# First layer's S5 preparation split into input operators and output tables in a two-layer hybrid backbone kernel

## The chip, the cores and the metric

One core of a Trainium2 (trn2) chip runs the whole kernel as one launch. The metric is the device time of a launch in microseconds (us). A core has TensorE (PE, with its weight loads listed apart as PEld), VectorE (DVE), ScalarE (ACT), GpSimd (POOL) and SyncE (SP); here SP issues every DMA. Each engine works through its own instruction stream in order.

## The reference

Two layers, each run over 640 tokens (128 context tokens and 512 latent ones), width 1024. A layer computes `h = x*(1+scale)+shift`, projects `h` to an S5 input `u`, to q/k/v of two attentions and to three gates, and merges three branches:

- branch A, a bidirectional S5: 32 groups of 16 channels, 64 complex states per group and direction, `state[t] = lam_bar*state[t-1] + b_bar*u[t]`, `y[t] = Re(c*state[t]) + d*u[t]`, both directions summed, then GELU and a gated linear unit. Context and latent tokens are separate sequences; the latent one starts from a given state.
- branch B, banded attention (distance up to 128, with a sink logit), 8 query heads on 2 key heads.
- branch C, global attention with RMS-normalised q and k.

`x = LayerNorm(alpha*x + gate1*(merged @ w_out))`, and then an MLP with squared ReLU of width 4096 and a second LayerNorm. Outputs are both token sets, the context's final S5 states and its keys and values.

## The kernel before, in words

**Matmuls.** Nearly all products are made from fp32r halves: `split` (L115 to L124) writes a high part on ACT (L123) and a low part on DVE (L124), and three matmuls make one product (`mm_fm` L159 to L161, `mm_tm` L170 to L172). Weights arrive as 512 KB tiles `raw` (four buffers, L114).

**Order of the work.** The kernel is written as one long program, but the tile framework is told to schedule it: a planner walks a simulated timeline, takes for each engine the instruction that is earliest in the program among those it believes ready, and so fixes each engine's order ahead of the run. The place in the program is therefore a priority. On the chip the order of an engine never changes; an instruction that is late holds everything behind it on its engine. Buffers of a pool tag (`bufs=`) are handed out in the same way.

**The S5 in chunks of 8 tokens.** There are 84 chunk columns (`NCH`). Per block of 4 groups (8 blocks) the kernel needs three tables that depend on the parameters alone: the *input operator* (8 tokens of `u` to a state increment), the *output table* `ct` (state to 8 tokens of `y`), and the *lag kernel* (`u` to `y` inside a chunk). `s5_prep` (L274) makes them:

- once: `lam_bar` and its powers 0 to 8 by some 130 DVE operations on 128x32, the factors `fr`, `fi`, and `ec`, `ei` (L400 to L405); loads of `dP` and `delta` (L407, L409). Then a `yield`.
- per block, first half (L413 to L471): `Bm`, `Cm` loaded by two DMAs (L419, L420); `Bb` by six DVE operations of 128x64 and a sign change of `Cm` (recorded at the helper lines L290 and L294); `ct` by six DVE operations of 128x512 (L445 to L447, L451 to L453), stored to DRAM (L454); `Bs`, a padded copy of `Bb`, by a POOL memset and three DVE copies (L457 to L460); 32 small matmuls (L465, L467) into a PSUM bank `p_pt` (two buffers); 16 columns of `KK` by DVE (L468), 128 by ACT (L469). Then a `yield`.
- per block, second half (L473 to L485): the input operator, six DVE operations of 128x512 (recorded at L290), eight PE transposes (L479), two ACT copies (L480). In layer 0 it is used at once (`s5_in`), in layer 1 stored to DRAM (`inop_d`). Then a `yield`.
- at the end: 8 DMAs of `KK` into `kk_d` (L487, L488), and 8 DMAs that turn `kk_d` into the lag tables `mg_d` (L490).

`s5_in` (L588): per block 2x4 matmuls (L596); ACT writes the forward half of the chunk states `st` (L598), DVE the reversed half in two copies (L600).

**Phase A of layer 0** (`phase_a`, L494): modulation, `h`, the `u` projection, with 8 steps of the preparation after tile 1 and 8 after tile 3 (`PREP`, L26, used at L628); then `kv_gemm(0)`, `q_gemm(0)`, `kv_gemm(1)`; `s5_states` (L633): pair sums on DVE (`pairs`, L660, L661), then a recurrence of 31 steps of four POOL operations (L677 to L680), pair sums again, reversal (L689 to L691); then the banded attention: `keys(0)`, and per 128 queries `attend` (scores L915 to L920, maximum L926, exponential L938, transposes L947, split, products L954 and L955). After it in the program: the q projection of the global attention (L785, L717 to L719), 7 tiles of gates ahead (`AHEAD`), the S5 output (L1016 to L1030: loads `mg` and `ct`, the latter as `tab` with three buffers, matmuls L1023 and L1025), and the rest of the phase. The queries of the next tile are split at L870 to L873.

**Layer 1** has its preparation made during the MLP of layer 0: `ahead` (52 calls in `up` and `down`) takes a step alternately of the modulation (25 steps with its last) and of `s5_prep` (18 with its last).

Of the kernel before, what the change touches and what calls it, by code (L numbers as in the profile page):

```python
# [24 lines left out]
UA = 3  # L25
PREP = (0, 8, 0, 8)  # L26
AFF = 0
# [3 lines left out]
def net(tc, I, O, depth=DEPTH, dbg=None):  # L31
# [221 lines left out]
    def hacts(h):  # L253
        return [tuple(tuple(z[:, k] for z in p) for p in h) for k in range(8)]
# [18 lines left out]

    def s5_prep(l, pp, after=None, use=None):  # L274
        pq = ppt
# [13 lines left out]
        def tt(o, a, b, op):  # L289
            V.tensor_tensor(o, a, b, op=op)  # L290
# [108 lines left out]

        ec = pp.tile([128, 2, 8, 32], F32, name=f"ec_{l}")  # L400
        ei = pp.tile([128, 2, 8, 32], F32, name=f"ei_{l}")
# [3 lines left out]
        V.tensor_copy(ei[64:128], Pw[64:128, :, 0:8, :])  # L405
        dP = pp.tile([128, 8], F32, name=f"dP_{l}")
        SY.dma_start(dP, I["ssm_d"][:, l])  # L407
        delta = pp.tile([128, 16], F32, name=f"delta_{l}")
        SY.dma_start(delta, I["delta"])  # L409
        KK = pp.tile([128, 8, 144], F32, name=f"KK_{l}")  # L410
        yield
        for b in range(8):
            gs = slice(4 * b, 4 * b + 4)  # L413

            def pt(name, shape, bufs=1):
                return pp.tile(shape, F32, name=name, tag=f"{name}_{l}", bufs=bufs)

            Bm, Cm = pt("Bm", [128, 2, 4, 16], 2), pt("Cm", [128, 2, 4, 16], 2)
            SY.dma_start(Bm, I["ssm_b"][l, :, :, gs])  # L419
            SY.dma_start(Cm, I["ssm_c"][l, :, :, gs])  # L420
            Bb, bt = pt("Bb", [128, 2, 4, 16]), pt("bt", [128, 4, 16])
            frb, fib = (f[:, gs].unsqueeze(2).to_broadcast([128, 4, 16]) for f in (fr, fi))
            tt(Bb[:, 0], Bm[:, 0], frb, ALU.mult)
            tt(bt, Bm[:, 1], fib, ALU.mult)
            tt(Bb[:, 0], Bb[:, 0], bt, ALU.subtract)
            tt(Bb[:, 1], Bm[:, 1], frb, ALU.mult)
            tt(bt, Bm[:, 0], fib, ALU.mult)
            tt(Bb[:, 1], Bb[:, 1], bt, ALU.add)
            ts(Cm[:, 1], Cm[:, 1], -1.0, None, ALU.mult)

            def vw(t, r_):
                return t[:, r_].unsqueeze(2).to_broadcast([128, 4, 8, 16])

            def ew(t, r_):
                return t[:, r_, :, gs].rearrange("p t g -> p g t").unsqueeze(3).to_broadcast([128, 4, 8, 16])

            def row():
                r = pp.tile([128, D], F32, name="prow", tag="row", bufs=3 if l else 6)
                return r.rearrange("p (r q t o) -> p r q t o", r=2, q=4, t=8)

            mm, ct = row(), row()
            m1, m2 = mm[:, 0], mm[:, 1]


            V.tensor_tensor(m1, vw(Cm, 0), ew(ec, 0), op=ALU.mult)  # L445
            V.tensor_tensor(m2, vw(Cm, 1), ew(ec, 1), op=ALU.mult)
            V.tensor_tensor(ct[:, 0], m1, m2, op=ALU.add)  # L447
            nn = row()
            n1, n2 = nn[:, 0], nn[:, 1]
            PE_ = V  # L450
            PE_.tensor_tensor(n1, vw(Cm, 1), ew(ec, 0), op=ALU.mult)  # L451
            PE_.tensor_tensor(n2, vw(Cm, 0), ew(ec, 1), op=ALU.mult)
            PE_.tensor_tensor(ct[:, 1], n1, n2, op=ALU.subtract)  # L453
            SY.dma_start(ctab_d[l][b], ct)  # L454

            Bs = pt("Bs", [128, 2, 4, 48])
            G.memset(Bs, 0.0)  # L457
            V.tensor_copy(Bs[:, :, :, 0:16], Bb)
            V.tensor_copy(Bs[0:64, :, :, 16:32], Bb[0:64])
            V.tensor_copy(Bs[64:128, :, :, 32:48], Bb[64:128])  # L460
            p = pq()
            for q in range(4):
                o = p[32 * q:32 * q + 32]
                for r_ in range(2):
                    T.matmul(o[:, 0:16], Bs[:, r_, q, 0:32], Cm[:, r_, q, :], start=(r_ == 0), stop=(r_ == 1))  # L465
                for r_ in range(2):
                    T.matmul(o[:, 16:144], Bs[:, r_, q, 16:48], ct[:, r_, q], start=(r_ == 0), stop=(r_ == 1))  # L467
            V.scalar_tensor_tensor(KK[:, b, 0:16], delta, dP[:, b:b + 1], p[:, 0:16], op0=ALU.mult, op1=ALU.add)  # L468
            S.activation(KK[:, b, 16:144], p[:, 16:144], AF.Copy)  # L469
            yield  # L470

            io = row().rearrange("p r q t o -> p r q (t o)")
            for r_ in range(2):  # L473
                tt(n1, vw(Bb, 0), ew(ei, r_), ALU.mult)
                tt(n2, vw(Bb, 1), ew(ei, 1 - r_), ALU.mult)
# [10 lines left out]
        for q in range(4):  # L486
            SY.dma_start(ap(kk_d[l], q * 3840 + 7 * 16, [[240, 16], [4 * 3840, 8], [1, 128]]), KK[32 * q:32 * q + 16, :, 0:128])  # L487
            SY.dma_start(ap(kk_d[l], q * 3840, [[240, 16], [4 * 3840, 8], [1, 112]]), KK[32 * q + 16:32 * q + 32, :, 32:144])  # L488
        for j in range(8):
# [3 lines left out]
    def phase_a(l, h):  # L493
        if l == 0:  # L494
            pp0 = tc.alloc_tile_pool(name="prep", bufs=1, side="right", reuse_waits="tile")
            s5_use = []
            prep = s5_prep(0, pp0, use=s5_use)
        qp = tc.alloc_tile_pool(name=f"qp{l}", bufs=1, reuse_waits="tile")
# [77 lines left out]
        st = sp.tile([128, NCH, 2, 32], F32, name="st")  # L576
        segs = ((0, 18), (18, 84))
        ubs = {}

# [8 lines left out]
        def s5_in(b, io):  # L588

            if b % 2 == 0:  # L590
                ubs[0] = load_u(b // 2)
            ub = ubs[0]
            for r_ in range(2):
                p = psc()
                for q in range(4):
                    T.matmul(p[:, q * NCH:(q + 1) * NCH], io[:, r_, q], ub[:, (b % 2) * 4 + q], start=True, stop=True)  # L596
                v = p[:, :4 * NCH].rearrange("p (g c) -> p c g", g=4)
                S.activation(st[0:64, 1:NCH, r_, 4 * b:4 * b + 4], v[0:64, 0:NCH - 1], AF.Copy)  # L598
                for a, e in segs:
                    V.tensor_copy(st[64:128, a + 1:e, r_, 4 * b:4 * b + 4], v[64:128, e - 1:a:-1])  # L600

# [31 lines left out]
        def s5_states():  # L633

            for b in range(8) if l > 0 else ():
                io = sp.tile([128, 2, 4, 128], F32, name="tab", tag="tab", bufs=3)
                SY.dma_start(io, inop_d[l][b])
                s5_in(b, io)
# [371 lines left out]
        for b in range(8):  # L1010
# [5 lines left out]
            SY.dma_start(mg, mg_d[l][:, 4 * b:4 * b + 4])  # L1016
            ct = sp.tile([128, 2, 4, 128], F32, name="tab", tag="tab", bufs=3)
            SY.dma_start(ct, ctab_d[l][b])
# [14 lines left out]
        T.matmul(fp[0:64, 0:128], fin, ident, start=True, stop=True)  # L1033
        fo = sp.tile([128, 1024], F32, name="fo", tag="tab", bufs=3)[0:64, 0:128]
        S.activation(fo, fp[0:64, 0:128], AF.Copy)
# [3 lines left out]
        SY.dma_start(yT, ap(y_d[l], 0, [[8 * NCH, 128], [128 * 8 * NCH, 4], [NCH, 8], [1, NCH]]))  # L1039
        atp[0].release()  # L1040
        sp.release()
        k0p.release()
# [122 lines left out]
    def phase_b(l, M):  # L1165
# [87 lines left out]
        for t in range(NT):  # L1253
# [6 lines left out]
            build_h(l, 1, h, t, x[:, t], mp)  # L1260
        h2 = hacts(h)
        nxt = []
        if l + 1 < depth:
            nxt = [mods_steps(l + 1, range(3), lambda: mp.tile([128, 512], F32, name="mtmp", tag="mtmp", bufs=1),
                              lambda: mp.tile([128, 4, 128], F32, name="hf", tag="hf", bufs=2).rearrange("p a b -> p (a b)")), s5_prep(l + 1, mp, x[:, NT - 1, D - 1:D])]
        calls = [0]
# [223 lines left out]
```

## Time and profile before

| what | us |
|---|---|
| median of three runs (lowest, highest) | 2383.68 (2381.09, 2385.68) |
| the profiled execution's own time | 2382.53 |
| its span, first to last instruction | 2380.7 |
| PE busy in the span | 2269.5 (95%) |
| DVE, ACT, POOL busy | 1493.8, 992.7, 159.8 |

The span and the profiled execution's time differ by 1.8 us of start and end. Shares are averages over stages with different limits; PE is the engine that is nearly always busy, and a stage is read by where PE stands idle or runs at a lower granted clock. Rows of later sections come from a trace of this execution, with times from the start of the span.

### The profile page before, as it was taken

To read this page: it belongs to the slowest core of one execution; us is meant where nothing else is said; L and a number is where in the kernel's file an instruction comes from. 1 tells how busy PE (TensorE), PEld (TensorE's weight loads), DVE (VectorE), ACT (ScalarE), POOL (GpSimd) and SP (SyncE) were. 2 spreads that over 40 slices of the span, in tenths; PEclk is the share of its full clock that TensorE was granted. 3 is DMA by queue.
4 is the path that set the end of the run, shared out by engine and by line. 5 is a ranking of instruction groups with operands and counts; after the bars stand their busy time and mean duration, and the time that the engine had idled before them with its cause. 6 is when DMAs were issued, how large, how long until landed. Compare 5 with 4: busy or idle time off the path is not lost.

```text
span 2380.7 us, 38633 instructions
## 1 busy us (share of the span) xinstructions
PE 2269.5 (95%) x14904; PEld 2061.5 (87%) x14904; DVE 1493.8 (63%) x3293; ACT 992.7 (42%) x2316; POOL 159.8 (7%) x323
## 2 busy tenths in 40 slices
PE   7987999999998999999999889999999899999997
PEld 4987896799987988887888889999999789988885
DVE  7887745775357766664675866466745863444468
ACT  3334655574244433222224256566643343322221
POOL 0005500000000000000000641000000000000000
PEclk8998999999999999999999999999999999999999
DMA  7533247522251354555336223522222522222221
GB/s 272 150 112 93 94 132 249 187 75 73 79 171 55 109 170 148 170 188 185 125 100 192 72 82 100 156 67 81 82 63 65 192 72 74 77 74 78 72 79 53
DMA packets 126360, 277.92 MB, mean 117 GB/s; under 512 B 40640, under 2 KB 60224, under 8 KB 126176
## 3 DMA queue, kind: packets, MB, share of 16 engines
q1 hardware_dynamic: 126176, 275.45, 36.6%
q8 instruction: 117, 1.92, 0.3%
q14 instruction: 67, 0.55, 0.1%
HBM read 240.97 MB, written 38.63 MB: 117 GB/s over the span
## 4 chain that ended last, share of the span: by engine, by line
PE 79%; DVE 8%; POOL 5%; DMA 4%; ACT 2%; issue 1%; SPq 1%; DVEq 0%; POOLq 0%; ACTq 0%
PE p_g L159 9%; PE p_g L160 9%; PE p_g L161 9%; PE p_sc L159 4%; PE p_sc L160 4%; PE p_sc L161 4%; PE p_sc L1204 4%; PE p_sc L1205 4%; PE p_sc L1206 4%; PE p_g L1204 2%; PE p_g L1205 2%; PE p_pt L947 2%; PE p_g L1206 2%; PE p_g L1025 2%; PE p_pv L955 1%; PE p_pv L954 1%
## 5 line engine op out<-in xcount | busy, mean ns | idle before, releaser
L124 DVE TENSOR_TENSOR wlo<-raw,whi 128x512 fp32r<-128x512 f32 x472 | 324.3, 692 | 277.0 <-ACT whi L123 269.1
L123 ACT ACTIVATE whi<-raw 128x512 fp32r<-128x512 f32 x472 | 294.0, 630 | 438.3 <-PE p_sc L1206 149.8
L159 PE MATMUL p_g<-hh,whi 128*128 128x256 f32 (+1 forms) x1224 | 383.4, 314 | 0.8 <-DVE rt L718 0.8
L160 PE MATMUL p_g<-hl,whi 128*128 128x256 f32 (+1 forms) x1224 | 382.6, 313 | 1.6 <-DVE hl L124 1.5
L161 PE MATMUL p_g<-hh,wlo 128*128 128x256 f32 (+1 forms) x1224 | 381.7, 312 | 0.2
L159 PEld LDWEIGHTS p_g<-hh,whi 128*128 128x128 f32 x1224 | 233.4, 191 | 7.4 <-ACT rl L1289 3.5
L160 PEld LDWEIGHTS p_g<-hl,whi 128*128 128x128 f32 x1224 | 233.7, 191 | 2.9 <-DVE hl L124 2.3
L161 PEld LDWEIGHTS p_g<-hh,wlo 128*128 128x128 f32 x1224 | 233.3, 191 | 1.3 <-DVE wlo L124 1.1
L160 PE MATMUL p_sc<-hl,whi 128*128 128x384 f32 (+1 forms) x648 | 202.0, 312 | 2.7 <-DVE hl L124 2.7
L159 PE MATMUL p_sc<-hh,whi 128*128 128x384 f32 (+1 forms) x648 | 202.5, 314 | 0.0
L161 PE MATMUL p_sc<-hh,wlo 128*128 128x384 f32 (+1 forms) x648 | 201.7, 311 | 0.0
L170 PE MATMUL p_g<-whi,hh 128*128 128x256 f32 x480 | 142.1, 297 | 12.6 <-DVE rt L718 5.9
L124 DVE TENSOR_TENSOR pl<-p_pt,ph 128x512 fp32r<-128x512 f32 (+1 forms) x176 | 103.2, 590 | 70.9 <-ACT ph L123 56.9
L171 PE MATMUL p_g<-wlo,hh 128*128 128x256 f32 x480 | 140.2, 294 | 5.4 <-DVE wlo L124 5.2
L159 PE MATMUL p_g<-act,whi 128*128 128x384 f32 x448 | 141.0, 315 | 4.2 <-ACT act L123 2.7
L172 PE MATMUL p_g<-whi,hl 128*128 128x256 f32 x480 | 139.1, 291 | 0.0
L160 PE MATMUL p_g<-act,whi 128*128 128x384 f32 x448 | 138.7, 310 | 0.3 <-DVE act L121 0.3
L161 PE MATMUL p_g<-act,wlo 128*128 128x384 f32 x448 | 138.8, 310 | 0.0
L1205 PE MATMUL p_sc<-wlo,ff 128*128 128x512 f32 x336 | 133.7, 398 | 0.0
L1204 PE MATMUL p_sc<-whi,ff 128*128 128x512 f32 x336 | 133.5, 398 | 0.0
L1206 PE MATMUL p_sc<-whi,ff 128*128 128x512 f32 x336 | 131.6, 394 | 0.0
L1290 DVE TENSOR_TENSOR rl<-rl 128x384 f32<-128x384 f32 (+1 forms) x128 | 62.2, 487 | 109.8 <-ACT rl L1289 109.3
(419 smaller groups left out, 5320.0 us busy)
## 6 DMA issues: line engine op xcount, KB each, us to landing
raw<-in_w_mod_dram SPq DMA_DIRECT2D x96, 512.0 KB
raw<-in_w_up_dram SPq DMA_DIRECT2D x64, 512.0 KB
raw<-in_w_down_dram SPq DMA_DIRECT2D x64, 512.0 KB
raw<-in_w_gate_dram SPq DMA_DIRECT2D x48, 512.0 KB
raw<-in_w_br_dram SPq DMA_DIRECT2D x24, 512.0 KB
raw<-in_w_q_dram SPq DMA_DIRECT2D x16, 512.0 KB
ctab_d<-prow SPq DMA_DIRECT2D x16, 512.0 KB
tab<-ctab_d SPq DMA_DIRECT2D x16, 512.0 KB
```

The source lines that it names most:

```text
L123: S.activation(hi, src, AF.Copy)
L124: V.tensor_tensor(lo, src, hi, op=ALU.subtract)
L159: T.matmul(out, wh, tok(ah, t0, t1), start=(first and k == 0), stop=False)
L160: T.matmul(out, wh, tok(al, t0, t1), start=False, stop=False)
L161: T.matmul(out, wl, tok(ah, t0, t1), start=False, stop=(last and k == n - 1))
L170: T.matmul(out, ah, wh, start=(first and k == 0), stop=False)
L171: T.matmul(out, ah, wl, start=False, stop=False)
L172: T.matmul(out, al, wh, start=False, stop=(last and k == n - 1))
L1204: T.matmul(banks[t], a_, wh, start=(k == 0), stop=False)
L1205: T.matmul(banks[t], a_, wl, start=False, stop=False)
L1206: T.matmul(banks[t], b_, wh, start=False, stop=(k == n - 1))
L1290: V.tensor_tensor(r[:, :n], r[:, :n], r[:, :n], op=ALU.mult)
```

## The change

`s5_prep` makes only the input operators now, and a new generator `s5_tables` the output tables and the lag kernel. In layer 0 the steps of `s5_tables` stand in the program in front of each query tile of the banded attention, four steps for a tile (two blocks), with a pool of their own (`tables`); in layer 1 they follow the input operators. `Bm` is loaded whole (one DMA of 512 KB) and `Bb` made for all groups by six operations of 128x512. The sign change of `Cm`, the copies into `Bs` and the reversed copies of `st` (both layers) go from DVE to ACT. `KK` is stored by 8 DMAs per block in place of 8 in all. `mm` and `ct` have one buffer each. `tab` has two buffers in layer 0. The SBUF that is kept for software DMA is cut (the kernel issues none from POOL).

```diff
-PREP = (0, 8, 0, 8)
+PREP = (0, 4, 0, 4)
...
-    def s5_prep(l, pp, after=None, use=None):
+    def s5_prep(l, pp, pl_, keep, after=None, use=None):
...
-        KK = pp.tile([128, 8, 144], F32, name=f"KK_{l}")
+        def row():
+            return pp.tile([128, D], F32, name="prow", tag="row", bufs=3)
+        Bm = row().rearrange("p (r g i) -> p r g i", r=2, g=32)
+        SY.dma_start(Bm, I["ssm_b"][l])
+        Bb = pl_.tile([128, 2, 32, 16], F32, name=f"Bb_{l}")
+        bt = row().rearrange("p (r g i) -> p r g i", r=2, g=32)
+        frb, fib = (f.unsqueeze(2).to_broadcast([128, 32, 16]) for f in (fr, fi))
+        tt(Bb[:, 0], Bm[:, 0], frb, ALU.mult)
...
         yield
         for b in range(8):
             gs = slice(4 * b, 4 * b + 4)
-            Bm, Cm = pt("Bm", [128, 2, 4, 16], 2), pt("Cm", [128, 2, 4, 16], 2)
...
+            n1, n2 = (z.rearrange("p (q t o) -> p q t o", q=4, t=8) for z in (lambda r: (r[:, 0:512], r[:, 512:1024]))(row()))
+            io = row().rearrange("p (r q c) -> p r q c", r=2, q=4)
             for r_ in range(2):
+                tt(n1, vw(Bb, 0, gs), ew(ei, r_, gs), ALU.mult)
+                tt(n2, vw(Bb, 1, gs), ew(ei, 1 - r_, gs), ALU.mult)
...
+        keep.update(Bb=Bb, ec=ec, dP=dP, delta=delta, vw=vw, ew=ew)
+
+    def s5_tables(l, pl_, keep):
...
+        for b in range(8):
+            gs = slice(4 * b, 4 * b + 4)
+            s4 = slice(0, 4)
+            Cm = pt("Cm", [128, 2, 4, 16], 2)
+            SY.dma_start(Cm, I["ssm_c"][l, :, :, gs])
+            S.activation(Cm[:, 1], Cm[:, 1], AF.Copy, scale=-1.0)
+            mm, ct = (pt(n, [128, 2, 4, 8, 16]) for n in ("mm", "ct"))
+            m1, m2 = mm[:, 0], mm[:, 1]
+            tt(m1, vw(Cm, 0, s4), ew(ec, 0, gs), ALU.mult)
...
+            tt(ct[:, 1], m1, m2, ALU.subtract)
+            SY.dma_start(ctab_d[l][b], ct)
+            Bs = pt("Bs", [128, 2, 4, 48])
+            G.memset(Bs, 0.0)
+            S.activation(Bs[:, :, :, 0:16], Bb[:, :, gs], AF.Copy)
+            S.activation(Bs[0:64, :, :, 16:32], Bb[0:64, :, gs], AF.Copy)
+            S.activation(Bs[64:128, :, :, 32:48], Bb[64:128, :, gs], AF.Copy)
+            yield
+            p = ppt()
...
+            KK = pt("KK", [128, 144], 2)
...
+            for q in range(4):
+                o = (4 * b + q) * 3840
+                SY.dma_start(ap(kk_d[l], o + 7 * 16, [[240, 16], [1, 128]]), KK[32 * q:32 * q + 16, 0:128])
+                SY.dma_start(ap(kk_d[l], o, [[240, 16], [1, 112]]), KK[32 * q + 16:32 * q + 32, 32:144])
+            yield
         for j in range(8):
             SY.dma_start(mg_d[l][16 * j:16 * j + 16], ap(kk_d[l], (7 - j) * 16, [[240, 16], [3840, 32], [1, 128]]))
...
+        TAB = 3 if l else 2
...
                 for a, e in segs:
-                    V.tensor_copy(st[64:128, a + 1:e, r_, 4 * b:4 * b + 4], v[64:128, e - 1:a:-1])
+                    S.activation(st[64:128, a + 1:e, r_, 4 * b:4 * b + 4], v[64:128, e - 1:a:-1], AF.Copy)
...
-        def attend_all(i, K, y):
+        def attend_all(i, K, y, side=iter(())):
             qs = qtile(i, 0)
             for t in range(NT):
                 nxt = qtile(i, t + 1) if t + 1 < NT else None
+                for _ in range(4):
+                    next(side, None)
                 attend(i, t, qs, *K, y)
...
-        attend_all(0, keys(0), yw)
+        tables = s5_tables(0, pl0, kept) if l == 0 else iter(())
+        attend_all(0, keys(0), yw, tables)
...
+        def both(l, pool, after):
+            kept = {}
+            yield from s5_prep(l, pool, pool, kept, after)
+            yield from s5_tables(l, pool, kept)
...
-    nc = bacc.Bacc("TRN2", target_bir_lowering=False, num_devices=1)
+    nc = bacc.Bacc("TRN2", target_bir_lowering=False, num_devices=1, dynamic_dma_scratch_size=1024)
```

## Rows read from the trace of the kernel before

**Rows 1.** Stretches by engine: window, length, busy us (count), PE clock, DMA share, GB/s.

```profile
core 0: us, PE busy (x) PEld busy (x) DVE busy (x) ACT busy (x) POOL busy (x), PEclk, DMA share, GB/s
0.00:60.00 60.00, 44.97 (x246) 28.92 (x246) 42.93 (x210) 19.80 (x39) 1.12 (x17) 0.89 0.80 271
15.00:25.00 10.00, 6.25 (x21) 4.00 (x22) 7.39 (x40) 4.52 (x10) 0.00 (x0) 0.50 1.04 400
60.00:160.00 100.00, 97.94 (x951) 94.85 (x950) 89.64 (x229) 36.26 (x107) 3.09 (x8) 1.00 0.47 136
160.00:180.00 20.00, 14.54 (x118) 13.26 (x118) 15.92 (x40) 4.47 (x23) 4.28 (x1) 0.77 0.41 107
...
190.00:210.00 20.00, 14.34 (x80) 13.14 (x79) 19.77 (x34) 9.52 (x33) 7.77 (x10) 0.83 0.30 95
210.00:250.00 40.00, 31.17 (x233) 30.21 (x232) 29.65 (x63) 17.93 (x80) 36.86 (x80) 0.91 0.14 47
250.00:357.00 107.00, 105.84 (x776) 99.93 (x777) 64.82 (x131) 64.46 (x154) 19.23 (x37) 1.00 0.39 119
...
700.00:1240.00 540.00, 531.17 (x3166) 450.94 (x3165) 350.00 (x809) 175.16 (x338) 7.01 (x16) 0.99 0.43 142
...
1290.00:1320.00 30.00, 29.49 (x256) 29.31 (x255) 11.85 (x36) 11.32 (x29) 0.21 (x1) 1.00 0.68 213
1330.00:1410.00 80.00, 65.36 (x502) 62.43 (x500) 57.07 (x106) 28.18 (x95) 62.40 (x125) 0.91 0.19 53
```

**Rows 2.** Timeline at 169.6 us: start, length, engine, operation [idle before, releaser].

```profile
169.44 0.21 DVE L459 COPY Bs<-Bb 64x128 f32<-64x128 f32 x1
...
169.75 0.21 PE L465 MATMUL p_pt<-Cm,Bs 128*32 128x16 f32 x2 [3.40 <-issue]
```

**Rows 3.** Waits, 160 to 250 us: who waited for whom, us in total, times, longest.

```profile
POOL sa L677 <- DMA st<-in_state_dram: 16.4, 1, 16.4
...
DVE ub L660 <- POOL st L680: 8.4, 2, 6.4
...
PE p_sc L915 <- DVE qs L872: 3.9, 1, 3.9
```

**Rows 4.** Groups of instructions, 0 to 310 us: count, busy us, mean ns, idle before.

```profile
L598 ACT ACTIVATE st<-p_sc 64x332 f32<-64x332 f32 x16 | 7.1, 441 | 19.0 <-PE p_sc L596 19.0
...
L600 DVE COPY st<-p_sc 64x68 f32<-64x68 f32 (+1 forms) x32 | 9.1, 328 | 7.7 <-ACT st L598 7.4
...
L445 DVE TENSOR_TENSOR prow<-Cm,ec 128x512 f32<-128x512 f32 x8 | 5.5, 685 | 0.0
...
L290 DVE TENSOR_TENSOR Bb<-Bb,bt 128x64 f32<-128x64 f32 x16 | 3.5, 218 | 0.0
...
L745 ACT ACTIVATE vf<-p_g 128x128 f32<-128x128 f32 x10 | 2.8, 280 | 0.0
...
L458 DVE COPY Bs<-Bb 128x128 f32<-128x128 f32 x8 | 1.8, 222 | 0.6 <-DVE Bb L290 0.5
...
L294 DVE TENSOR_SCALAR Cm<-Cm 128x64 f32<-128x64 f32 x8 | 1.4, 192 | 5.4 <-DMA Cm<-in_ssm_c_dram 5.4
```

**Rows 5.** Timeline of the recurrence on POOL, and of DVE beside it.

```profile
204.17 1.14 DVE L660 TENSOR_TENSOR ub<-st,lam 128x704 f32<-128x704 f32 x1
...
204.65 0.99 POOL L677 TENSOR_TENSOR sa<-st,l 128x128 f32<-128x128 f32 x1
...
217.57 0.46 POOL L677 TENSOR_TENSOR sa<-st,l 128x128 f32<-128x128 f32 x1
...
223.20 0.83 DVE L660 TENSOR_TENSOR ub<-st,lam 128x640 f32<-128x640 f32 x1 [6.38 <-POOL st L680]
```

**Rows 6.** Timeline of SP's DMA issues.

```profile
66.22 0.33 SPq L1018 DMA_DIRECT2D tab<-ctab_d  x1
...
175.23 0.43 SPq L487 DMA_DIRECT2D kk_d<-KK  x1
...
177.41 6.77 SPq L490 DMA_DIRECT2D mg_d<-kk_d  x8
```

More of the change, by code (lines that the diff above doesn't have):

```diff
@@ L398, in s5_prep @@
         tt(fi, fi, den, ALU.mult)
-        ec = pp.tile([128, 2, 8, 32], F32, name=f"ec_{l}")
+        ec = pl_.tile([128, 2, 8, 32], F32, name=f"ec_{l}")
         ei = pp.tile([128, 2, 8, 32], F32, name=f"ei_{l}")
@@ L405, in s5_prep @@
         V.tensor_copy(ei[64:128], Pw[64:128, :, 0:8, :])
[L406 removed]
+        dP = pl_.tile([128, 8], F32, name=f"dP_{l}")
         SY.dma_start(dP, I["ssm_d"][:, l])
[L408 removed]
+        delta = pl_.tile([128, 16], F32, name=f"delta_{l}")
         SY.dma_start(delta, I["delta"])
[L410 removed]
+        def row():
+            return pp.tile([128, D], F32, name="prow", tag="row", bufs=3)
@@ L411, in s5_prep, with vw, ew @@
+        tt(bt[:, 1], Bm[:, 0], fib, ALU.mult)
+        tt(Bb[:, 1], Bb[:, 1], bt[:, 1], ALU.add)
         yield
+        def vw(t, r_, gs):
+            return t[:, r_, gs].unsqueeze(2).to_broadcast([128, 4, 8, 16])
+        def ew(t, r_, gs):
+            return t[:, r_, :, gs].rearrange("p t g -> p g t").unsqueeze(3).to_broadcast([128, 4, 8, 16])
         for b in range(8):
             gs = slice(4 * b, 4 * b + 4)
-            def pt(name, shape, bufs=1):
-                return pp.tile(shape, F32, name=name, tag=f"{name}_{l}", bufs=bufs)
@@ L426, in s5_prep @@
[L426 to L467, printed above, removed]
@@ L494, in phase_a @@
         if l == 0:
+            pl0 = tc.alloc_tile_pool(name="tables", bufs=1, side="right", reuse_waits="tile")
+            kept = {}
             pp0 = tc.alloc_tile_pool(name="prep", bufs=1, side="right", reuse_waits="tile")
             s5_use = []
-            prep = s5_prep(0, pp0, use=s5_use)
+            prep = s5_prep(0, pp0, pl0, kept, use=s5_use)
         qp = tc.alloc_tile_pool(name=f"qp{l}", bufs=1, reuse_waits="tile")
@@ L635, in s5_states @@
             for b in range(8) if l > 0 else ():
-                io = sp.tile([128, 2, 4, 128], F32, name="tab", tag="tab", bufs=3)
+                io = sp.tile([128, 2, 4, 128], F32, name="tab", tag="tab", bufs=TAB)
                 SY.dma_start(io, inop_d[l][b])
@@ L994, in phase_a @@
         yw = qw[:, 0:2560].rearrange("p (t f n) -> p t f n", t=NT, f=4)
-        attend_all(0, keys(0), yw)
+        tables = s5_tables(0, pl0, kept) if l == 0 else iter(())
+        attend_all(0, keys(0), yw, tables)
+        for _ in tables:
+            pass
         dump("yw", qw[:, 0:2560])
@@ L1016, in phase_a @@
             SY.dma_start(mg, mg_d[l][:, 4 * b:4 * b + 4])
-            ct = sp.tile([128, 2, 4, 128], F32, name="tab", tag="tab", bufs=3)
+            ct = sp.tile([128, 2, 4, 128], F32, name="tab", tag="tab", bufs=TAB)
             SY.dma_start(ct, ctab_d[l][b])
@@ L1033, in phase_a @@
         T.matmul(fp[0:64, 0:128], fin, ident, start=True, stop=True)
-        fo = sp.tile([128, 1024], F32, name="fo", tag="tab", bufs=3)[0:64, 0:128]
+        fo = sp.tile([128, 1024], F32, name="fo", tag="tab", bufs=TAB)[0:64, 0:128]
         S.activation(fo, fp[0:64, 0:128], AF.Copy)
@@ L1040, in phase_a @@
         atp[0].release()
+        if l == 0:
+            pl0.release()
         sp.release()
@@ L1264, in phase_b @@
             nxt = [mods_steps(l + 1, range(3), lambda: mp.tile([128, 512], F32, name="mtmp", tag="mtmp", bufs=1),
-                              lambda: mp.tile([128, 4, 128], F32, name="hf", tag="hf", bufs=2).rearrange("p a b -> p (a b)")), s5_prep(l + 1, mp, x[:, NT - 1, D - 1:D])]
+                              lambda: mp.tile([128, 4, 128], F32, name="hf", tag="hf", bufs=2).rearrange("p a b -> p (a b)")), both(l + 1, mp, x[:, NT - 1, D - 1:D])]
         calls = [0]
```

37 lines of the change are left out of this document (21 added, 16 removed).

## The prediction

> **What bounds the kernel now.** I read the page first (PE is busy 95% of the span, so only time in which PE idles or runs slowly can be won), then the busy time by stretches, then the timeline and the waits of the stretch that stood out.
>
> The reader is to see in [rows 1] three kinds of stretch. From 60 to 160 us PE is busy 97.94 of 100 us, though DVE, at 89.64, is nearly full too: PE bounds, with DVE close behind. From 250 to 357 us PE is busy 105.84 of 107. Between them lies the hole. In 160 to 180 PE idles 20 - 14.54 = 5.46 us at a mean granted clock of 0.77, in 190 to 210 5.66 us at 0.83, in 210 to 250 8.83 us at 0.91. The granted clock is one of two levels, 2.4 GHz or 1.2 GHz, so a mean of 0.77 is a stretch partly at half speed, right behind an idle PE; the busy time would have been shorter at full clock by busy x (1 - clock): 3.3, 2.4 and 2.8 us. Together the three stretches lose 8.8 + 8.1 + 11.6 = 28.5 us.
>
> What ends the waits there: at 169.75 us PE starts the small table matmul of the last block after 3.40 us of idling, 0.10 us after DVE ended the copy into `Bs` that it reads (169.44 + 0.21) [rows 2]; the engines are in order, so the q projection, ready or not, stood behind it. In 190 to 210 DVE is busy 19.77 of 20 us and PE waits 3.9 us at once for `qs`, which DVE makes [rows 1, 3]. In 210 to 250 DVE itself stands still: 8.4 us in two waits for the recurrence on POOL, the longest 6.38 us [rows 3, 5]. So the first two losses are DVE backlog that the preparation left behind, and the third is not.
>
> **The change, step by step.** Sums go against the profiled execution, 2382.5 us (its span, 2380.7, and 1.8 around it). The median of the runs, 2383.7, is 1.2 higher, which I add at the end.
>
> *DVE work.* Moved: the six 128x512 operations of `ct`, 6 x 8 x 0.685 = 32.9 us [rows 4] (L446 to L453 have the same duration). Taken off DVE: 48 operations of 128x64 for `Bb`, about 48 x 0.218 = 10.5 us, against six of 128x512, 4.1 us; the sign change, 1.4 us; copies into `Bs`, about 24 x 0.22 = 5.3 us; reversed copies of `st`, 9.1 us [rows 4]. Net -22 us for good, and 33 us with a lower priority.
>
> *60 to 160 us.* PE does the same matmuls, and DVE falls from 89.64 [rows 1] by about seven eighths of 55 us, to some 42, before tables are put back as filling. PE can gain at most its 2.06 us of idling; I take -1 (bounds 0 and -2.1).
>
> *160 to 180 us.* No table matmul stands in PE's queue in front of the q projection with a DVE that is a block behind. I take all of it, -8.8 (bounds 0 and -8.8).
>
> *190 to 210 us.* The pair sums (L660, L661) and the key splits met here because the last `s5_in` came late. With the input operators first they are done earlier, but attention's own splits stay. I take half, -4 (bounds 0 and -8.1).
>
> *210 to 250 us.* What is late next is the recurrence: its 31 x 4 POOL operations are untouched. I take 0; the bounds are -11.6 (it now runs wholly under the earlier projections) and +25 (third rival).
>
> Layer 1 is a check on these four: there no preparation runs in the phase, and 1330 to 1410, where its recurrence runs, still loses 14.64 us of idling and 65.36 x 0.09 = 5.9 of clock, 20.5 us [rows 1], 8 less than layer 0's 28.5.
>
> *Start.* `Bm` whole is 0.52 MB ahead of `x` on SP. DMA moves 400 GB/s in 15 to 25 us at a share of 1.04 [rows 1]: +1.3 us if `x` waits for it, less what the first block's table operations no longer take from DVE. I take +1 (bounds -2 and +1.3).
>
> *Two `tab` buffers.* A third load is no longer ahead. Six loads of 0.52 MB, 1.3 us each at the rate above, are the most, +7.9; gates and attention lie between the blocks (PE 105.84 of 107 [rows 1]) and hide nearly all. +1 (bounds 0 and +7.9).
>
> *ACT.* 32 copies of `st` (nearest row: the forward half, 0.441 us), 24 into `Bs` (0.28 us), 8 sign changes: up to 14.1 + 6.7 + 2.2 = 23 us [rows 4]. ACT is busy 36.26 of 100 us [rows 1], whose idle time hides it: 0. Without that cover the bank `p_sc` would come free up to 0.9 us later in each of 16 uses, +14. Layer 1's 32 copies lie in 1290 to 1320, PE 29.49 of 30 and ACT 11.32: 0 (bounds -2 and +2).
>
> *SP.* 8 loads of `Bm` become one, and 8 stores of `KK` become 64: 56 x 0.43 = 24 us more of issuing [rows 6]. A store waits for ACT's part of `KK`, and behind it in SP's queue stand weight loads; these have four buffers, so a wait of some us reaches no matmul: 0 (bounds 0 and +5). SP also waits long today without PE showing it.
>
> *New waits.* `ct` has one buffer: a block's first write of it waits for the store of the block before, and DVE's attention work is queued behind, for which ACT and PE wait. Blocks that the planner places over tens of us don't meet; at the worst 7 waits of about one store, 1.3 us by the rate above: +9, taken 0. The lag tables (6.77 us of issues [rows 6]) end later, in front of the fourth query tile at the latest; the S5 output is late if PE runs out of gates by then: within the bounds of the third rival.
>
> *Layer 1's preparation.* 26 steps for 18, with modulation's 25 that is 51 of 52 calls, so it ends just inside the MLP. PE is busy 531.17 of 540 us there and DVE 350 [rows 1]; the matmuls hide it: 0 (bounds -2 and +4: SP's 24 us again, four weight buffers deep).
>
> Sum: -1 - 8.8 - 4 + 0 + 1 + 1 = -11.8, to 2370.7 of the profiled execution, 2372 of a median.
>
> **Rivals.** 0.2% is 4.8 us, about what a measurement of this kernel can tell from no change.
>
> *More than that (0.18).* The recurrence moves so far ahead that attention never waits for it: another -11.6 and the other half of 190 to 210, -4: 2356. For it: POOL stood idle for 16.4 us waiting for the state's load behind the pair sums [rows 3], and the pair sums were late because of DVE. Against it: layer 1's 20.5 us.
>
> *The change doesn't do what it says (0.16).* Where a step stands in the program is only a priority. The planner already issued a load of the S5 output at 66.22 us, though it stands in the program behind the whole banded attention [rows 6]. It can put the tables back between the projections, where DVE seems free to it. As filling that is harmless, but if DVE is full again there, each block is shorter by only 22/8 = 2.7 us, the last table matmul still holds PE, and -2.7 + 2 is no change: 2383.
>
> *The tables block the recurrence (0.16), slower.* A POOL operation of 128x128 takes 0.99 us beside a DVE operation with both inputs in SBUF and 0.46 alone [rows 5]: +0.53. The 48 table operations are of that kind. If all lie beside the recurrence it lasts 48 x 0.53 = 25 us longer; the planner doesn't know, DVE stands in order at the pair sums for it, and PE lost about one for one there (8.83 idle for 8.4 waited [rows 1, 3]). That gives 2372 + 25 = 2397; it decides from 23 table operations on (12/0.53). For it: the change puts them beside attention, which is where the recurrence was. Against: in 60 to 160 us DVE will have room for them, and the planner fills room. The Trainium skill (SBUF — State Buffer, "Who interferes with whom") states that a DVE instruction with two SBUF inputs and a GpSimd instruction that reads SBUF exclude each other for the length of an instruction; the rows agree, and by that rule this change is a risk where its own words promise cover.
>
> *Other losses (0.08).* SP's queue or the lag tables late, +10 to +15 on the forecast: about 2385.
>
> **How the numbers follow.** The forecast's own case (0.42) is -5 to -20. Faster: 0.42 + 0.18 = 0.60. No change: 0.16. Slower: 0.16 + 0.08 = 0.24. The range reaches a little past the best case, to 2353, and a little short of the worst, to 2393; the forecast's own range is 2364 to 2379.
>
> **What the profile after would show.** Right: PE idle in the 20 us after `kv_gemm(1)` mostly gone, no small table matmul with an idle PE before it, DVE well under 90% while the projections run, the first POOL operation of the recurrence before 190 us, the S5 output's last matmul some 12 us before 357. Wrong: DVE waits for POOL longer than 12 us in all, POOL operations of 128x128 mostly near 1 us, or PE waiting for `mg`. A loss in the MLP of layer 0 or in layer 1 would make the prediction wrong from a side where I put nothing.

## The result, and the profile after

The changed kernel takes 2413.14 us (median of four runs, 2410.81 to 2416.18) beside 2383.34 for the kernel before: a ratio of 1.0119, interval 1.0107 to 1.0132. It is 28 to 30 us **slower**; 2372 was forecast, and the range ended at 2393. The profiled execution has a span of 2409.0 us.

Busy time by stretches after, with the columns of [rows 1]. The last three answer to its layer stretches, 27 us later.

```profile
core 0: us, PE busy (x) PEld busy (x) DVE busy (x) ACT busy (x) POOL busy (x), PEclk, DMA share, GB/s
...
60.00:160.00 100.00, 96.36 (x814) 93.56 (x813) 76.15 (x142) 49.26 (x132) 11.64 (x17) 0.98 0.32 94
160.00:180.00 20.00, 16.50 (x131) 15.31 (x129) 14.52 (x26) 8.23 (x33) 18.98 (x30) 0.83 0.27 84
180.00:200.00 20.00, 6.48 (x32) 4.79 (x30) 14.78 (x28) 4.37 (x17) 18.75 (x36) 0.66 0.18 61
...
210.00:250.00 40.00, 37.59 (x312) 34.72 (x312) 31.55 (x64) 26.94 (x95) 9.57 (x30) 0.91 0.33 107
250.00:310.00 60.00, 60.00 (x500) 55.80 (x499) 43.94 (x91) 34.90 (x105) 9.90 (x4) 1.00 0.33 110
310.00:340.00 30.00, 24.45 (x172) 20.74 (x171) 15.03 (x34) 14.45 (x39) 0.00 (x0) 0.89 0.52 157
340.00:397.00 57.00, 52.58 (x353) 50.95 (x352) 15.48 (x29) 18.25 (x42) 0.00 (x0) 0.88 0.58 178
727.00:1267.00 540.00, 531.36 (x3159) 452.59 (x3158) 339.47 (x730) 182.75 (x369) 6.95 (x16) 0.99 0.42 142
1317.00:1347.00 30.00, 29.87 (x258) 29.70 (x257) 2.05 (x3) 18.88 (x61) 0.21 (x1) 1.00 0.73 228
1357.00:1437.00 80.00, 68.62 (x513) 65.58 (x511) 57.92 (x107) 28.36 (x96) 62.01 (x125) 0.89 0.17 56
```

Layer 1 and the MLP lose nothing: PE idles 8.64 us of 540 (8.83 before), and the stretch of layer 1's recurrence is a little better. The loss is made by 400 us: the load of `yT` behind the S5 output is issued at 398 us instead of 366. Two stretches are new. From 180 to 200 PE is busy 6.48 of 20 us, at a clock of 0.66. From 310 to 397 it idles 5.55 + 4.42 us and runs at 0.88 to 0.89, where [rows 1] show 105.84 busy of 107 at full clock for 250 to 357.

**The second stretch: late lag tables.** SP's queue on the timeline (start, length, engine, line, operation, [idle before, releaser]):

```profile
312.63 0.37 SPq L478 DMA_DIRECT2D ctab_d<-ct  x1
313.51 0.30 SPq L498 DMA_DIRECT2D kk_d<-KK  x1
...
316.64 0.42 SPq L499 DMA_DIRECT2D kk_d<-KK  x1
317.10 0.42 SPq L829 DMA_DIRECT2D s_d<-gt  x1
317.69 5.97 SPq L502 DMA_DIRECT2D mg_d<-kk_d  x8
...
328.19 0.80 SPq L1036 DMA_DIRECT2D mg<-mg_d  x2
```

PE on the timeline, with its wait for the first load of `mg`:

```profile
327.87 0.28 PE L935 MATMUL p_sc<-maskb,identb 128*128 128x256 bf16 x1
331.20 0.42 PE L1043 MATMUL p_g<-ub,mg 128*128 128x84 f32 x2 [3.04 <-DMA mg<-mg_d]
```

Before, `mg_d` was issued at 177.41 [rows 6] and the S5 output ran from 294 to 358 us as filler between the softmax steps. Now `mg_d` is issued 140 us later, and the output runs from 331 to 391, behind an attention that had no filler from 310 on.

**The first stretch: three engines in a chain.** The timeline there, DVE, POOL and PE:

```profile
183.81 0.38 PE L969 MATMUL p_pv<-ph,VV 128*128 128x256 f32 x1 [0.30 <-ACT ph L123]
...
185.10 1.98 POOL L766 TENSOR_TENSOR ksq<-ksq,mh 128x10 f32<-128x10 f32 x1
...
187.12 0.94 DVE L767 TENSOR_TENSOR kf<-kf,ksq 128x640 f32<-128x640 f32 x1 [2.82 <-POOL ksq L766]
...
187.97 0.93 DVE L676 TENSOR_TENSOR st<-st,ub 128x640 f32<-128x640 f32 x1
...
188.83 0.94 DVE L675 TENSOR_TENSOR ub<-st,lam 128x640 f32<-128x640 f32 x1
...
190.09 0.41 DVE L124 TENSOR_TENSOR pl<-p_pt,ph 128x256 fp32r<-128x256 f32 x1
...
190.55 0.58 PE L970 MATMUL p_pv<-pl,VV 128*128 128x256 f32 x1 [6.37 <-DVE pl L124]
```

The power for the keys' norm stands in POOL's order inside the recurrence. DVE waits 2.82 us for it, does the norm and pair sums, and only then the split that PE has waited for 6.37 us. The waits of 150 to 250 us (who waits for whom: us, times, longest) show more of it:

```profile
ACT Bs L482 <- POOL Bs L481: 15.2, 3, 7.9
...
DVE ub L675 <- POOL st L695: 12.1, 4, 5.1
```

DVE stands 12.1 us for the recurrence (8.4 before [rows 3]), and ACT 15.2 us for a memset that POOL runs between recurrence operations.

To compare runs below I use PE's *excess*, worked out from every matmul of a trace: the time from its start to the next matmul's start, less the 30th percentile of that spacing behind matmuls of the same line and shape, where it is longer, summed by stretch (us). It holds idling and low clock alike; what is left of the span is nearly the same in all (2079 to 2087 us), and least in notab and dveonly, which have no small table matmuls in layer 0. Work shifts between stretches, so sums count most.

```
           0-60  60-150  150-250  250-400  400-600   600-    sum
before     25.0     9.3     37.1     31.1     28.2  144.2  274.9
after      28.7     9.8     41.8     36.6     37.3  145.6  299.8
mgprobe    28.8    11.8     41.2     25.3     26.6  147.0  280.7
mgct       28.3    10.8     41.0     25.3     32.1  144.3  281.8
dveonly    28.1    11.4     29.1     32.0     24.5  145.3  270.4
notab      25.5     8.3     25.5     38.5     19.1  144.7  261.6
early16    28.9     9.1     54.0     24.6     36.5  150.5  303.6
chain      27.4    12.0     52.6     27.6     41.8  148.1  309.5
nosplit    29.1    18.3     35.4     26.9     35.4  146.5  291.6
```

Of the 28.3 us that the span grew, 24.9 are excess.

### The profile page after: what moved, and what is told of

It reads as the page before. It is cut to its first block, busy times and chain, and to the rows that moved or that the text cites. A ratio compares the mean times of both kernels' runs of the same rounds, so it can differ in the third digit from the quotient of the medians.

```text
span 2409.0 us, 38688 instructions
## 1 busy us (share of the span) xinstructions
PE 2289.3 (95%) x14904; PEld 2076.7 (86%) x14904; DVE 1460.4 (61%) x3081; ACT 1024.7 (43%) x2444; POOL 165.8 (7%) x323
## 4 chain that ended last, share of the span: by engine, by line
PE 82%; DVE 5%; POOL 5%; DMA 3%; ACT 2%; issue 1%; SPq 1%; DVEq 0%; ACTq 0%; POOLq 0%
PE p_g L159 10%; PE p_g L161 10%; PE p_g L160 9%; PE p_sc L159 4%; PE p_sc L160 4%; PE p_sc L161 4%; PE p_sc L1226 4%; PE p_sc L1227 4%; PE p_sc L1228 4%; PE p_pt L962 2%; PE p_g L1226 2%; PE p_g L1227 2%; PE p_g L1228 2%; PE p_g L170 2%; PE p_g L171 2%; PE p_g L172 2%
## 5 line engine op out<-in xcount | busy, mean ns | idle before, releaser
L159 PEld LDWEIGHTS p_sc<-hh,whi 128*128 128x128 f32 x648 | 124.2, 192 | 6.4 <-ACT rl L1316 4.2
```

Source lines behind the costliest of these rows:

```text
L159: T.matmul(out, wh, tok(ah, t0, t1), start=(first and k == 0), stop=False)
```

## The experiments

Ratios are to the kernel before, measured beside each run; 0.001 is 2.4 us.

**mgprobe** takes the wait for the lag tables away.

```diff
-            SY.dma_start(mg, mg_d[l][:, 4 * b:4 * b + 4])
+            SY.dma_start(mg, mg_d[l][:, 4 * b:4 * b + 4] if l else I["w_u"][1, b % 4][:, 0:512].rearrange("p (a c) -> p a c", a=4))
```

> The changed kernel, but in layer 0 the S5 output reads its lag matrices from a weight that lies in DRAM from the start, so that it waits for no lag table (the tables, their stores and mg_d are still made; the values of the SSM branch are others). Theory A (late lag tables: the tables end at 317 us, mg is issued at 317.7 to 323.7, and the S5 output then runs behind the attention instead of inside it): S5 output starts before 305 us, and the time falls by 18 to 26 us, to 2387 to 2395. Theory B (DVE stands behind the recurrence on POOL from 180 to 210 and that hole is the loss): the hole stays, the time stays at 2408 or more. Theory C (two tab buffers in layer 0 make the S5 output crawl): it starts earlier but ends near 385 us all the same, time 2405 or more.

2389.94 us, ratio 1.0025 (1.0015 to 1.0034). The time is as theory A said, 23 us less, though the S5 output started at 309, not before 305. From 310 to 340 PE is full again, and the hole of 150 to 250 stays:

```profile
150.00:250.00 100.00, 74.08 (x603) 68.12 (x603) 78.53 (x148) 47.42 (x186) 66.41 (x129) 0.83 0.27 86
...
310.00:340.00 30.00, 30.00 (x247) 28.59 (x246) 13.81 (x28) 14.99 (x38) 0.00 (x0) 1.00 0.72 233
```

**early16, skip0, chain, chainu** make the tables earlier, in four ways.

```diff
 early16, skip0:
-                for _ in range(4):
+                for _ in range(16):                      # early16
+                for _ in range(16 if t == 1 else 0):     # skip0
 chain, chainu: s5_tables drawn behind s5_prep by the same iterator, none in attend_all; chainu also
-PREP = (0, 4, 0, 4)
+PREP = (0, 4, 0, 20)
```

> The changed kernel with 16 table steps instead of 4 drawn ahead of each query tile, so that all of them stand ahead of query tile 0 in the program. A: mg_d is issued before 260 us, the S5 output starts before 305, time 2388 to 2400. B: 33 us of table work fall on the stretch of the recurrence, DVE and POOL slow each other, the hole of 180 to 210 grows by 5 to 10 us and eats a part: 2400 to 2420. C: 2405 to 2413.

> The changed kernel with no table step ahead of query tile 0 and all 16 ahead of query tile 1. Theory A+D: mg_d comes at about 270 us instead of 317, and the tables stay out of the recurrence's first half: S5 output starts before 320, the excess from 150 to 250 is 42 to 50 us, time 2395 to 2405. If only lateness counts: 2390 to 2395. If only crowding counts: 2405 to 2415.

> The changed kernel with its table steps drawn right behind the input operators, by the same projections that drew the preparation before, none beside the attention. A: mg_d is issued before 230 us and nothing of the 30 us is lost; with the DVE work that is gone the time is 2365 to 2383. B: the tables meet the recurrence earlier and the hole in front of the attention stays or grows, 2383 to 2405. C: 2395 or more, since two tab buffers stay.

> The changed kernel with every table step drawn in the projections of u, behind the input operators, where the whole preparation was drawn before (the run that drew them in the projections behind gave 2414.5 and had the hole between 150 and 250 us grow to 52 us). Theory A': table work costs nothing only as long as it lies in the stretch to 160 us in which PE has a queue of ready matmuls; then mg_d is issued by 200 us, the hole from 150 to 250 is at most the 37 us of before, and the time is 2370 to 2384. Theory E (input operators first bring the recurrence forward into the table work, wherever the tables are drawn): 2390 or more.

| run | us | ratio (interval) | `mg_d` issued at | excess 150 to 250 |
|---|---|---|---|---|
| early16 | 2407.83 | 1.0098 (1.0076 to 1.0121) | 262 | 54.0 |
| skip0 | 2404.29 | 1.0078 (1.0061 to 1.0095) | 281 | 41.7 |
| chain | 2414.50 | 1.0127 (1.0112 to 1.0142) | 245 | 52.6 |
| chainu | 2417.61 | 1.0134 (1.0118 to 1.0150) | 243 | 53.2 |

`mg_d` is issued earlier, and in three of the four runs the hole at 150 to 250 grows by about as much as that gives back: early tables crowd what stands around the recurrence. skip0, which keeps out of its first half, keeps the hole as it was and is the best of them. The S5 output still starts late, at 316, 303, 314 and 311 us (294 before), so the lag tables are not all that it stands behind. chain and chainu missed A's numbers by 30 us. In them the attention itself begins only at 249 and 247 us (156 in the changed kernel), and in chain PE idles 23.7 us between 150 and 250 right in front of small table matmuls. chainu draws its table steps in the projections of `u`, yet the planner put the small matmuls at 131 us and later all the same, behind all input operators.

**notab, dveonly, mgct** were meant to part that crowding. All read both of the S5 output's tables from weights; mgct makes every table step, dveonly the 48 DVE operations with `Cm` and the stores of `ct` alone, notab none.

```diff
-            SY.dma_start(ct, ctab_d[l][b])
+            SY.dma_start(ct, ctab_d[l][b] if l else I["w_u"][1, 3 - b % 4].rearrange("p (r a c) -> p r a c", r=2, a=4))
 mg as in mgprobe; dveonly, behind the store of ct:
+            if l == 0:
+                yield
+                yield
+                continue
 notab:
-        tables = s5_tables(0, pl0, kept) if l == 0 else iter(())
+        tables = iter(())
```

> The changed kernel without layer 0's table steps at all (48 VectorE operations, the small matmuls, KK, its stores and mg_d are left out; the S5 output reads both tables from weights in DRAM, so the SSM branch has other values). It tells what the table steps cost in all in their new place, and what is left without them. Theory A+D (the tables are the whole loss: late ones stall the S5 output, early ones crowd VectorE beside the recurrence): the hole at 180 to 210 closes, the excess of PE from 150 to 250 falls from 41.8 to some 25 us, time 2362 to 2376. Theory B (the recurrence brought forward makes the hole: VectorE waits for POOL with the attention behind it): the hole stays, 150 to 250 keeps 35 us or more, time 2380 to 2390.

> The changed kernel with every table step still made, but the S5 output of layer 0 reads both its tables (lag and output) from weights in DRAM, so it waits for none of them (other values in the SSM branch). With the lag tables alone read from a weight the time was 2389.9. If waiting for the output tables (the last is stored at 313 us) costs too: 2380 to 2386. If what is left is crowding of the attention by the table steps: 2387 to 2391.

> As mgct, and of layer 0's table steps only the 48 operations on VectorE, the loads and sign of Cm and the stores of ct are left (no Bs, no small matmuls, no KK, no 64 stores, no mg_d). If the 48 operations are the crowding: 2383 to 2390, close to mgct, and 14 to 20 us above the run without any table step (2369.4). If the small matmuls in PE's queue, KK and the queue's issues are it: 2369 to 2375.

notab: 2369.35 us, 0.9938 (0.9919 to 0.9957). dveonly: 2374.54, 0.9961 (0.9947 to 0.9976). mgct: 2394.13, 1.0040 (1.0027 to 1.0054). The stretch 150 to 250 by engines, of notab:

```profile
150.00:250.00 100.00, 87.97 (x628) 82.91 (x628) 76.02 (x158) 60.56 (x220) 58.47 (x112) 0.91 0.23 69
```

Of dveonly:

```profile
150.00:250.00 100.00, 82.42 (x616) 77.66 (x612) 81.51 (x154) 57.39 (x215) 61.23 (x126) 0.93 0.21 68
```

And of mgct:

```profile
150.00:250.00 100.00, 73.27 (x608) 67.69 (x607) 79.17 (x149) 47.10 (x187) 64.18 (x127) 0.86 0.25 83
```

This gives two prices, from the ratios. Waiting for the tables costs 0.0079, 19 us (from mgct to the changed kernel). All table steps, made in their new place with nobody waiting for them, cost 0.0102, 24 us (from notab to mgct). Together that is 43 us. mgct beside mgprobe shows that waiting for the output tables costs nothing, and that two plans can differ by 4 us without a reason that I can name.

dveonly lies 0.0023, 5 us (with a scatter of some 6), above notab and 0.0079, 19 us, below mgct, and its time is in the range of its second expectation. But it doesn't part the 24 us by kind of step, because its 48 operations are not beside the attention: without the small matmuls the planner put 47 of them ahead of 150 us, where mgct has 8. DVE with the table operations alone (L461; us, DVE busy (count), PE clock, DMA share, GB/s), of dveonly:

```profile
0.00:150.00 150.00, 30.98 (x47) 0.92 0.60 193
```

And of mgct:

```profile
0.00:150.00 150.00, 5.25 (x8) 0.93 0.52 167
```

So the 5 us are the price of the operations among the projections, where the kernel before has them too. The 19 us hold both the rest of the steps (`Bs`, the small matmuls, `KK`, its stores and `mg_d`) and the move of 39 DVE operations into the stretch of the recurrence and the attention. Some of it is also plain work of PE. The instructions that write or read `Bs` keep PE busy 11.57 us in mgct, with 256 small matmuls:

```profile
0.00:400.00 400.00, 11.57 (x256) 8.16 (x256) 6.53 (x24) 3.33 (x8) 0.94 0.47 152
```

In the kernel before (PE, PEld, DVE and POOL) it is 9.85 us:

```profile
0.00:400.00 400.00, 9.85 (x256) 7.61 (x256) 4.58 (x24) 3.36 (x8) 0.95 0.49 154
```

**bsonce, bsearly** test the memset that ACT waits for: one `Bs`, zeroed once in the preparation; bsearly also draws 8 table steps a tile.

```diff
-            Bs = pt("Bs", [128, 2, 4, 48])
-            G.memset(Bs, 0.0)
 in s5_prep, behind Bb:
+        Bs = pl_.tile([128, 2, 4, 48], F32, name=f"Bs_{l}")
+        G.memset(Bs, 0.0)
```

> The changed kernel with one Bs tile that is zeroed once, in the preparation, instead of once a block; the zero parts are never written over. Theory F (the zeroing stands in POOL's order inside the recurrence, ScalarE waits for it in front of its Bs copies, 15.2 us between 150 and 250, and the copies of kf and the exponentials stand behind): no wait of ScalarE for POOL's Bs, excess of 150 to 250 from 41.8 to 28 to 33 us, 2398 to 2405; the lag tables stay late, so most of the 23 us stay. If the crowding is the small matmuls and KK themselves: 2409 to 2414.

> bsonce with 8 table steps instead of 4 ahead of each query tile, so that the tables end with query tile 1. F and A together: the tables no longer block ScalarE beside the recurrence, so they may be early: mg_d by 265 us, S5 output not waiting for mg, 2376 to 2390. If the early tables crowd by something else: 2395 to 2408, as the 2407.8 of the run with 16 steps.

2411.28 us, 1.0108 (1.0093 to 1.0123), and 2411.06, 1.0114 (1.0097 to 1.0131). Theory F fell. bsonce's ACT no longer waits for POOL, and the waits of 150 to 250 have another link in its place:

```profile
DVE ub L675 <- POOL st L695: 12.2, 4, 5.1
...
ACT KK L495 <- DVE KK L494: 9.8, 2, 8.6
```

The copy of `KK` on ACT waits 8.64 us at 181.82 for the DVE half; DVE stood 5.07 us at a pair sum ahead of it. The wait that was longest was a symptom: taking one link away moved it to the next. The excess of 150 to 250 is 41.9, as before the edit. bsearly issued `mg_d` at 268 us, as meant, and there this excess is some 51.

**nosplit, nosplit2** undo the split alone.

```diff
 nosplit: PREP = (0, 12, 0, 12), and one iterator for both
+                for b in range(8):
+                    yield next(tabs)
+                    yield next(tabs)
+                    yield next(ops)
 nosplit2: also ct computed in place with one temporary, and
+ct = pt("ct", [128, 2, 4, 8, 16], 2 - l)
```

> The changed kernel with the split undone: per block first the two table steps, then the input operator, all drawn in the projections of u as before. What stays of the change: Bb in six whole operations, the small copies on ScalarE, ct in one buffer, KK per block, two tab buffers. If the split is the whole loss: 2365 to 2384, 28 us or more under the changed kernel. If the other parts cost (buffers, the queue): 2390 to 2405.

> The kernel with the split undone (2398.0), with two buffers for ct in layer 0 (room from computing ct in place with one temporary of half the size). If the one ct buffer costs the 9 us of 60 to 150: the excess there falls from 18.3 to 9 to 11 us and the time to 2385 to 2391. If not: 2395 to 2401.

2397.96 us, 1.0057 (1.0040 to 1.0074), and 2402.05, 1.0069 (1.0054 to 1.0084). The split is half of the loss, 15 us. With `mg_d` at 168 us the lag tables are not late, yet 13 us stay, 9 of them from 60 to 150; a second `ct` buffer beside the undone split (nosplit2) doesn't give them back.

**tab3h, kkone, bmlate** try three small terms: three `tab` buffers (with `ct` in place), `KK` in one tile with 8 stores, and `Bm` behind the loads of `x`. kkone, too, computes `ct` in place.

```diff
 tab3h:  -TAB = 3 if l else 2   +TAB = 3
 kkone:  -KK = pt("KK", [128, 144], 2), 8 stores a block   +KK = pl_.tile([128, 8, 144], ...), 8 stores at the end
 bmlate: a yield ahead of Bm = row()..., PREP = (0, 5, 0, 4)
```

> The changed kernel with three tab buffers in layer 0 as before (the room comes from computing ct in place, with one temporary of half the size; same number of operations). Theory A (late lag tables): the S5 output still waits for mg and starts near 330 us, but its two-buffer crawl of 370 to 390 eases: 0 to -6 us, 2407 to 2413. Theory C (two tab buffers are the loss): 2390 or less.

> The changed kernel with the lag kernel gathered in one tile and stored by 8 transfers at the end, as before, instead of 64. If the 56 more issues on the DMA queue (some 0.46 us each, 25 us in all) delay the lag tables and the loads behind them: -4 to -10 us, 2403 to 2409. If the queue has room (my sum's 0): -3 to 0, 2410 to 2413.

> The changed kernel with the whole Bm load (0.52 MB) and Bb taken one step later, behind the loads of x and of the first weights, instead of in front of x. PE's excess from 0 to 60 us is 28.7 against 25.0 before. If the load in front of x costs those 3.7 us: 2408 to 2411. If it is the tile planner's other order: 2412 to 2415.

tab3h 2421.89 us, 1.0157 (1.0140 to 1.0174); kkone 2413.28, 1.0122 (1.0107 to 1.0137); bmlate 2414.05, 1.0121 (1.0106 to 1.0136). None gives anything back; tab3h is even slower, why is open. bmlate's excess of 0 to 60 is 29.5: the load in front of `x` isn't what that stretch lost.

**pooltab** is nosplit2 with the 48 operations on POOL.

```diff
-            V.tensor_tensor(o, a, b, op=op)
+            (V if l else G).tensor_tensor(o, a, b, op=op)
```

> nosplit2 with the 48 table operations of layer 0 on POOL, which stands idle until the recurrence, instead of VectorE. If VectorE is what both placements crowd: 33 us leave it, the tables are done by 160 us, 2368 to 2382, under the kernel before. If POOL's operations are too slow (at 0.99 us for 128x128 beside VectorE, a 128x512 one could take 2 to 4 us, 96 to 190 us in all) or slow VectorE: 2390 to 2430.

2407.99 us, 1.0091 (1.0068 to 1.0113): no faster than on DVE (1.0069; the intervals overlap). POOL needs 1.32 to 1.59 us for each on the mean, and PE idles 16 of 90 us from 60 to 150, where it idles 7 in nosplit2 and 2 in the kernel before.

**stact, actall**: the kernel before with the small copies of the change.

```diff
-                    V.tensor_copy(st[64:128, a + 1:e, r_, 4 * b:4 * b + 4], v[64:128, e - 1:a:-1])
+                    S.activation(st[64:128, a + 1:e, r_, 4 * b:4 * b + 4], v[64:128, e - 1:a:-1], AF.Copy)
 actall: also the copies into Bs and the sign of Cm
```

> The kernel before with one part of the change: the reversed copies of st on ScalarE instead of VectorE. If these copies only relieve DVE: -4 to 0 us, 2379 to 2384. If ScalarE's slower copies delay the S5 input or the splits (theory D): 2386 to 2395.

> The kernel before with all the small copies of the change on ScalarE (st, Bs and the sign of Cm), nothing moved. The st copies alone gave 2380.4 against 2384.3. If VectorE bounds the preparation, the other 6.7 us of its work add a little: 2375 to 2380. If ScalarE's copies delay something: 2381 to 2386.

2380.41 us, 0.9986 (0.9976 to 0.9995), and 2380.30, 0.9978 (0.9969 to 0.9987). Both **beat both kernels**, the one before by 3 to 5 us. The rows of stact that answer to [rows 1]:

```profile
160.00:180.00 20.00, 16.16 (x167) 14.54 (x168) 13.96 (x26) 7.51 (x30) 2.55 (x2) 0.91 0.76 207
190.00:210.00 20.00, 16.67 (x101) 16.23 (x101) 15.20 (x29) 7.67 (x32) 18.82 (x31) 0.83 0.25 77
```

9 us less on DVE, and PE is busy 1.6 and 2.3 us longer in the two stretches where DVE was the last to end.

## Why the prediction was wrong

**The step that failed** is *New waits*: "The lag tables … end later, in front of the fourth query tile at the latest; the S5 output is late if PE runs out of gates by then", priced at nothing, and in the rivals at +10 to +15 with a chance of 0.08. The condition was right and so was the place: the last table matmuls ran at 312 us, PE ran out, and waiting cost 19 to 23 us. I had not seen that the S5 output was itself the filler of the attention's last third, the stretch that [rows 1] show at 105.84 of 107.

The same step has the wrong reader for `ct`. It lets a block's first write of the one buffer wait for the store of the block before, "about one store, 1.3 us". The small matmuls read `ct` as well, and they come late: the first block's `ct` was stored at 68.27 us, but its matmuls start at 155.95, just behind the first scores of the attention, for PE was busy with projections (96.36 of 100 us from 60 to 160). The next block's two products were made at 71.40; its first write of `ct` stands behind those matmuls. DVE and PE on the timeline:

```profile
71.40 1.29 DVE L461 TENSOR_TENSOR mm<-Cm,ec 128x512 f32<-128x512 f32 x2
...
155.95 0.30 PE L490 MATMUL p_pt<-Cm,Bs 128*32 128x16 f32 x4
...
160.62 0.68 DVE L461 TENSOR_TENSOR ct<-mm 128x512 f32<-128x512 f32 x1
```

In all seven later blocks this write starts 0.2 to 5.6 us behind the end of the last small matmul of the block before. In dveonly, where the store is the only reader, DVE waits for it 4.5 us in all and the tables are stored by 153 us. So the one buffer and the matmuls' place in PE's order go with the lateness; that they alone make it is not shown, since no run has the split with two buffers of `ct`.

**The second failure** has no term at all: what the table steps cost in their new place when nobody waits for them, 24 us from notab to mgct. Up to 11.57 us of it is PE's own time with the small matmuls, most of which the kernel before spends as well (9.85 us), so some 12 us are left, as an estimate. I had put the `ct` operations "with a lower priority" at nothing beside the attention, and had not priced `Bs`, the 32 matmuls and both halves of `KK` as instructions in the ordered queues of POOL, ACT, PE and DVE. Which of the two the 12 us belong to stays open, because dveonly took away the one and moved the other. That stalls are coupled through these queues is argued from the waits, not shown: bsonce took one link out for nothing, PE in mgct waits only 0.2 us in front of small matmuls, and in dveonly the planner also began the attention at 172 us, 18 later than in mgct. A run with the matmuls but without `KK` wasn't tried.

Point by point:

- *60 to 160, -1*: PE is busy 1.6 us less, at a clock of 0.98: a small loss, outside the bounds of 0 and -2.1. DVE did fall, to 76.15, as the tables came in mostly from 160 on.
- *160 to 180, -8.8, and 190 to 210, -4*: wrong. A table matmul again starts behind an idle PE (2.13 us at 165.68), and 180 to 200 alone loses 13.5 us of idling and 6.48 x 0.34 = 2.2 of clock. notab does gain: its excess of 150 to 250 is 11.6 less than before, though without any small matmuls.
- *210 to 250, 0*: loses 2.41 + 3.4 = 5.8 for 11.6; the recurrence did move forward, to 148 us.
- *Start, +1*: the excess rose by 3.7, but not by `Bm` (bmlate). Runs with other plans have 25 or 29.
- *Two `tab` buffers, ACT, SP, `ct`'s buffer*: taken at 1, 0, 0 and 0, and tab3h, kkone and nosplit2 gave nothing back. nosplit2 has the split undone, so `ct`'s buffer beside the split stays untested. ACT's copies of `st` are even the one part that pays (stact).
- *Layer 1*: right, in all three rows.

**The rivals.** *The tables block the recurrence* had the right sign for another reason. The recurrence on POOL lasts 71.6 us for 68.7 before, 3 us more and not 25. POOL's groups from 120 to 330 us show that only the first operation of a step averages 1.00 us:

```profile
L692 POOL TENSOR_TENSOR sa<-st,l 128x128 f32<-128x128 f32 x8 | 8.0, 1000 | 10.9 <-DMA st<-in_state_dram 10.3
L693 POOL TENSOR_TENSOR sb<-st,l 128x128 f32<-128x128 f32 x8 | 5.3, 667 | 0.0
L694 POOL TENSOR_TENSOR sa<-sa,st 128x128 f32<-128x128 f32 x8 | 5.1, 641 | 0.0
```

The exclusion of the Trainium skill (SBUF — State Buffer, "Who interferes with whom") is visible on both sides, for `ct`'s operations beside POOL last up to 0.94 us for 0.685, but it is small here. *The change doesn't do what it says* had a part: what decides is where the planner puts a step. chainu shows that the program's place alone doesn't bring it forward, and in dveonly the planner put the operations back among the projections, as that rival has it. Of the signs named as wrong, two came: DVE waits for POOL 12.1 + 2.8 = 14.9 us, and PE waits for `mg`.

The gain side is neither confirmed nor refuted. notab, with no table step of layer 0, takes 2369.4 us where 2372 was forecast, 15 us under the kernel before; but it also spares PE the small matmuls, which the forecast kept. With their 9.85 us put back, as an estimate, 5 us of gain could be left of the 12 that were forecast.

**Open:** which steps the 12 us belong to; whether two buffers of `ct` would bring the tables forward; what the 13 us of nosplit are; why tab3h is slower; and why the changed kernel and the plans of early tables lose 5 to 14 us more than the kernel before from 400 to 600.

## What to carry to other kernels

Before a group of steps is moved to a lower priority, name who reads its last result, and whether that reader is itself the work that fills a later stretch: a late table costs nothing until the filler that needs it is the only one left. Follow a moved step through every engine queue that it passes, and name every reader of each of its buffers: here small matmuls stood 88 us behind their `ct` in the order of PE, the engine that always had other work, and the next block stood behind them in the one buffer. When a run leaves some steps out, look where the planner put the rest before the difference is called a price. And when the longest wait is taken away and the time stays, look for the next link: in ordered queues the wait shown is often where a stall surfaced, not where it began.

## What the hardware showed unexpectedly

ACT makes the reversed copies of `st` about as fast as DVE: 0.370 and 0.222 us for 64x260 and 64x68 (296 ns on the mean), where DVE took 328 ns on the mean [rows 4]. A POOL operation of 128x512 beside a busy DVE took 1.32 to 1.59 us, less than the 2 to 4 us that I had put up from the 128x128 ones.
